# Trainium2 study: one branch removed between two layers, three adaLN blocks moved, one scatter replaced by one-hot products

## The chip, the cores and the metric

The kernel runs on one core of one Trainium2 chip. The metric is the device time of one execution in microseconds. The kernel before takes 1316.8 us (median of three runs, 1316.08 to 1317.06).

## What is computed

Two layers of a post-norm backbone over 256 context tokens and 256 latent tokens, width 1024. Each layer modulates its stream with adaLN vectors, projects it once to 4096 columns, feeds two head groups (a two-way gated linear recurrence, HGRN2, and a neighbourhood attention), projects back, normalises, and sends every token to 2 of 16 experts:

```python
def grouped_moe(h, w_router, b_router, w_gate_l, w_up_l, w_down_l):
    ...
    combine = jnp.sum(jax.nn.one_hot(e_idx, N_EXPERTS, dtype=f32) * gates[..., None], axis=1)
    out = jnp.zeros((n, shp[-1]), f32)
    for e in range(N_EXPERTS):
        hid = jax.nn.silu(t @ w_gate_l[e]) * (t @ w_up_l[e])
        out = out + combine[:, e:e + 1] * (hid @ w_down_l[e])
...
for l in range(DEPTH):
    mod_lat = (silu_c @ w_ada[l] + b_ada[l])[:, None, :]
    ...
    u_lat = (x_lat * (1.0 + sc1) + sh1) @ w_in[l]
    ...
    x_lat = layer_norm(ALPHA * x_lat + g1 * y_lat, ln1_g[l], ln1_b[l])
    f_lat = grouped_moe(x_lat * (1.0 + sc2) + sh2, ...)
    x_lat = layer_norm(ALPHA * x_lat + g2 * f_lat, ln2_g[l], ln2_b[l])
    ...
```

All data is float32. Layer 0 computes context and latent tokens (512), layer 1 the latent output alone (256).

## The kernel before

**A layer.** `run` calls `layer(l)` for l = 0 and 1. `layer` calls `front` (input projection, recurrence, attention, output projection), then `moe`, and for layer 0 `combine`, which gathers the experts' outputs, updates the stream `x`, normalises it, and writes layer 1's input (`xh`, `xl`). A list scheduler reorders the instructions of each engine; the source order and data dependences are what it starts from.

**The front.** The projection is cut into 16 chunks of 256 output columns. One chunk's weights are one load of 1 MB (`wload`, L199), issued on SP into a tile of the pool tag `w8`. That tag has three tiles (NWP = 3), handed out in turn. A loaded chunk is split in four pieces of 128x512 into a high part `wh` (ACT, L421) and a low part `wl` (L422, on POOL, or on DVE where the table SPL says V), and multiplied in three passes (xh·wh, xl·wh, xh·wl: L426, L427, L428, tiles `pscm` or `pstm`). A chunk has two units of 24 passes. Between the chunks stand pieces of the recurrence (`hgB` L727, `hgX` L744) and of the attention (`ats` L881, `atp` L901, `ato` L912).

**The adaLN blocks.** The adaLN vectors of both layers need 48 blocks of weights, 1 MB each. `fill(n)` computes the next n of them at a chosen chunk: eight calls on TensorE (L377, tile `psada`, 16 passes of 128x256 in the trace), a copy on ACT (L380), two small products (L384, `ptada`) and two small DVE instructions (L395, which write `ada`). In the front the blocks' weights go through the same three `w8` tiles. FILL0 and FILL1 are tables of n by chunk. Six blocks (NADA) of layer 1 that layer 0's front has left over are loaded at the end of layer 0's expert phase (L1486, tiles `wa`) and computed in one `fill(NADA, True)` behind the last expert.

**The experts.** Experts come in order 0 to 15. `gu(e, k0)` and `gu(e, k1)` are the two halves of gate and up (L1369, `pgA`), `htrans` transposes the hidden tile (L1394, `pth`), `down(e)` multiplies by the second matrix (L1406, `pdA`) and evicts the result to `y` (ACT L1419). POOL then scatters the rows of `y` to the DRAM buffer `yD` with an indirect DMA (L1433), two rows for each token. Weights stream in 1 MB loads through 16 slots (7 `we`, 3 `w8`, 6 `mw`).

**The layer's end.** If some expert has more tokens than its slots, a flag is read into a register and `If(fv)` (L1531) branches to `overflow`. The branch stands on every engine after each layer. Only then come `combine`'s loads of `yD` (L1555, eight of 512 KB on SP). For each of the eight y tiles `pair` weights one of a token's two rows on ACT (L1579) and adds the other on DVE (L1580). TensorE transposes the sums (L1568, `ptf`), DVE adds them to x (L1570), TensorE sums squares and means (L1052, `st`), POOL takes the power for the standard deviation (L1072), TensorE spreads it, and DVE normalises (L1086, L1087).

## Time and profile before

| what | value |
|---|---|
| median of the runs | 1316.8 us |
| profiled execution | 1317.83 us, of it the span 1316.1 us |
| TensorE busy in the span | 1199.3 us, 91% |
| VectorE, ScalarE, GpSimd busy | 45%, 31%, 25% |
| mean granted clock of TensorE | 0.958 |
| DMA | 339.32 MB, 258 GB/s over the span |

The profiled execution takes 1.73 us more than its span, which is what lies around the instructions that the profile shows, and 1.03 us more than the median of the runs. TensorE is busy for nine tenths of the time, so what matters are the places where it is not, and the stretches in which its work stands on the path to the end.

### The profile page before, as it was taken

The page shows a single profiled execution, that of the slowest core. Times are in us where ns is not written, and L with a number is a line of the kernel's source. Part 1 is how long each engine was busy: PE and PEld are TensorE (multiplying, and loading weights), DVE is VectorE, ACT ScalarE, POOL GpSimd, SP SyncE. Part 2 cuts the span into 40 slices and gives each one's busy share as a digit, 9 for nine tenths or more (in the row PEclk, how much of TensorE's full clock was granted, in tenths as well). Part 3 has the DMA queues.
Part 4 walks back from the last instruction along what each step waited for, and adds up shares of the span by engine and source line. Part 5 has one row for each costly group of instructions (what it writes and reads, how often), then busy time and mean ns, then how long its engine had stood idle before and what let it go on. Part 6 is the DMA issues. An engine that isn't in the chain of part 4 may idle for free. (4 is left out here: it accounts for less than half of the span.)

```text
span 1316.1 us, 22763 instructions
## 1 busy us (share of the span) xinstructions
PE 1199.3 (91%) x8919; PEld 747.6 (57%) x8919; DVE 590.2 (45%) x1397; ACT 413.8 (31%) x905; POOL 334.4 (25%) x349
## 2 busy tenths in 40 slices
PE   6989999988999799998997999998889899999984
PEld 4778767667788334333332688876667734333321
DVE  2466554786735414121111756364785524322214
ACT  2233254452544114111112653354345312001011
POOL 2233243323223101111000534353343311111001
PEclk9999999999999799999998999998999889999996
DMA  8794325313385799999998524354335799999993
GB/s 299 250 313 189 122 89 197 116 52 108 124 332 188 266 374 375 386 395 384 412 404 298 227 101 167 115 192 152 131 116 213 314 352 380 389 404 402 421 413 151
DMA packets 67684, 339.32 MB, mean 258 GB/s; under 512 B 10003, under 2 KB 17907, under 8 KB 31856
## 3 DMA queue, kind: packets, MB, share of 16 engines
q1 hardware_dynamic: 54016, 315.74, 62.1%
q0 software_dynamic: 5936, 12.58, 2.9%
q10 hardware_dynamic: 7616, 9.44, 2.2%
q8 instruction: 74, 1.21, 0.4%
q14 instruction: 42, 0.34, 0.1%
HBM read 322.80 MB, written 20.45 MB: 261 GB/s over the span
## 5 line engine op out<-in xcount | busy, mean ns | idle before, releaser
L422 POOL TENSOR_TENSOR wl<-w,wh 128x512 fp32r<-128x512 f32 x121 | 166.4, 1389 | 188.5 <-ACT wh L421 171.7
L1369 PE MATMUL pgA<-we,xgT 128*64 128x512 f32 x688 | 165.2, 613 | 2.7 <-DMA we<-in_wgu_dram 2.7
L426 PE MATMUL pscm<-xh,wh 128*128 128x512 f32 (+1 forms) x320 | 119.1, 376 | 3.3 <-ACT wh L421 2.3
L427 PE MATMUL pscm<-xl,wh 128*128 128x512 f32 (+1 forms) x320 | 120.7, 379 | 0.7 <-POOL xl L1603 0.5
L428 PE MATMUL pscm<-xh,wl 128*128 128x512 f32 (+1 forms) x320 | 118.6, 375 | 2.8 <-POOL wl L422 2.6
L421 ACT ACTIVATE wh<-w 128x512 fp32r<-128x512 f32 x160 | 96.5, 626 | 50.4 <-PE pscm L427 18.7
L1369 PEld LDWEIGHTS pgA<-we,xgT 128*64 128x64 f32 x688 | 48.1, 140 | 95.1 <-issue 84.9
L427 PE MATMUL pstm<-wl,xh 128*128 128x256 f32 x320 | 92.6, 290 | 3.4 <-DVE wl L422 1.8
L428 PE MATMUL pstm<-wh,xl 128*128 128x256 f32 x320 | 91.9, 287 | 0.0
L426 PE MATMUL pstm<-wh,xh 128*128 128x256 f32 x320 | 91.6, 287 | 0.0
L1433 POOL DMA_INDIRECT yD<-y,ss x25 | 23.0, 921 | 244.6 <-DVE y L1421 79.9
L1406 PE MATMUL pdA<-we,hdT 128*64 128x512 f32 x320 | 77.6, 619 | 3.3 <-DMA we<-in_wd_dram 3.2
L1369 PE MATMUL pgA<-mw,xgT 128*64 128x512 f32 x336 | 77.5, 598 | 0.0
L1360 DVE COPY xgT<-ptx 128x256 f32<-128x256 f32 (+1 forms) x32 | 15.4, 482 | 134.2 <-PE ptx L1354 91.1
L426 PEld LDWEIGHTS pscm<-xh,wh 128*128 128x128 f32 x320 | 61.3, 193 | 13.8 <-ACT wh L421 2.4
L428 PEld LDWEIGHTS pscm<-xh,wl 128*128 128x128 f32 x320 | 61.5, 193 | 12.5 <-POOL wl L422 3.4
L427 PEld LDWEIGHTS pscm<-xl,wh 128*128 128x128 f32 x320 | 61.9, 194 | 11.2 <-POOL xl L1603 1.6
L1387 DVE SCALAR_TENSOR_TENSOR hid<-hid,pgA 128x256 f32<-128x256 f32 x32 | 13.5, 421 | 115.2 <-ACT hid L1386 115.1
L427 PEld LDWEIGHTS pstm<-wl,xh 128*128 128x128 f32 x320 | 61.4, 192 | 5.4 <-POOL wl L422 2.2
L1386 ACT ACTIVATE hid<-pgA 128x256 f32<-128x256 f32 x32 | 12.3, 383 | 159.5 <-PE pgA L1369 159.5
L428 PEld LDWEIGHTS pstm<-wh,xl 128*128 128x128 f32 x320 | 61.5, 192 | 1.1 <-issue 0.8
L426 PEld LDWEIGHTS pstm<-wh,xh 128*128 128x128 f32 x320 | 61.4, 192 | 0.5
(394 smaller groups left out, 2358.9 us busy)
## 6 DMA issues: line engine op xcount, KB each, us to landing
we<-in_wgu_dram SPq DMA_DIRECT2D x86, 1024.0 KB
mw<-in_wgu_dram SPq DMA_DIRECT2D x42, 1024.0 KB
w<-in_wada_dram SPq DMA_DIRECT2D x41, 1024.0 KB
we<-in_wd_dram SPq DMA_DIRECT2D x40, 1024.0 KB
w<-in_win_dram SPq DMA_DIRECT2D x29, 1024.0 KB
mw<-in_wd_dram SPq DMA_DIRECT2D x24, 1024.0 KB
w<-in_wout_dram SPq DMA_DIRECT2D x11, 1024.0 KB
wa<-in_wada_dram SPq DMA_DIRECT2D x6, 1024.0 KB
```

Source lines behind the costliest of these rows:

```text
L421: self.nc.scalar.activation(hi, src, AF.Copy)
L422: leng.tensor_tensor(lo, src, hi.bitcast(F32), op=ALU.subtract)
L426: mm(out, lh, rh, start=first, stop=False, **k)
L427: mm(out, lh, rl, start=False, stop=False, **k)
L428: mm(out, ll, rh, start=False, stop=last, **k)
L1360: V.tensor_copy(t[:, 0:4, :c], src)
L1369: mm(pA[64 * j:64 * j + 64, :], xgT[e][:, k, 0:64], wk[:, 512 * j:512 * j + 512], start=(k == 0), stop=(k == KT - 1), skip_group_check=Tru ...
L1386: S.activation(h, ps[:, :n], AF.Tanh, scale=0.5)
L1387: V.scalar_tensor_tensor(h, h, 1.0, ps[:, :n], op0=ALU.add, op1=ALU.mult)
L1406: mm(dA[64 * j:64 * j + 64, :], hdT[e][:, kb, 0:64], wk[:, 512 * j:512 * j + 512], start=(kb == 0), stop=(kb == 3), skip_group_check=True, ...
L1433: G.indirect_dma_start(out=self.yD[l][:], out_offset=bass.IndirectOffsetOnAxis(ap=idx, axis=0), in_=y[:c], in_offset=None, bounds_check=2 ...
```

## The change

The change has five parts.

1. `layer(0)` no longer reads its flag or branches. The flag is kept in `over`, merged with layer 1's, and one `If` at the end of the program reruns both layers on the slow path (not taken with these inputs).
2. FILL0 rises from 2 to 3 at chunks 8, 11 and 13, and behind layer 0's experts NAFTER = 3 blocks are computed where NADA = 6 were. The three weights tiles there are now `we` tiles.
3. `early` now holds for layer 0 too: expert 14's second matrix is loaded before the second half of expert 15's first, and `down(14)` stands ahead of `gu(15, k1)`.
4. Expert 15's 64 rows of layer 0 aren't scattered. They are weighted by their gate on ACT and DVE (`yh`, `yl`, L1430 and L1431 of the changed kernel), and `pair` adds them through 16 products of 128x512 with a one-hot matrix `place` (`pz`, L1636). `last_slots` builds `place` while expert 13 is computed. The addition in `pair` becomes: DVE L1638 (eight, one operand from PSUM), DVE L1643 (six), ACT L1640 (two) and POOL L1641 (two).
5. `pairs_load`, the eight loads of `yD`, is issued ahead of `down(15)`; it depends on the scatters of experts 0 to 14 alone. `pair(1, 1)` stands ahead of `end(0)`.

```diff
+NAFTER = 3
-FILL0 = (0, 0, 0, 2, 2, 2, 2, 0, 2, 0, 2, 2, 0, 2, 0, 2)
+FILL0 = (0, 0, 0, 2, 2, 2, 2, 0, 3, 0, 2, 3, 0, 3, 0, 2)
...
+        with tc.If(self.fv):
+            self.slow = True
+            self.x = [self.xtile(h) for h in range(2)]
+            for l in range(2):
+                self.l = l
+                self.layer(l)
...
+            if l == 0 and e == NE - 1:
+
+                yh, yl = self.yparts = [self.rt([P, 512], "hr", 4, F32R) for _ in range(2)]
+                S.activation(yh[:], dA[:], AF.Copy, scale=self.slots[:, 0:1])
+                V.scalar_tensor_tensor(yl[:], dA[:], self.slots[:, 0:1], yh[:].bitcast(F32), op0=ALU.mult, op1=ALU.subtract)
+                return
...
-            early = l == 1 and e == NE - 2
+            early = e == NE - 2
...
-                for i in range(NADA):
-                    if i < NWP:
-                        w = self.wp.tile([P, 2048], F32, tag="w8", name="wa")[:]
-                    else:
-                        w = ep.tile([P, 2, 1024], F32, tag="mw", bufs=NMW, name="wa").rearrange("p a b -> p (a b)")
-                    nc.sync.dma_start(w, self.A["wada"][self.todo[i][:2]])
-                    self.todo[i] = self.todo[i][:2] + (w,)
+                for i in range(NAFTER) if self.todo else ():
+                    t = self.todo[i][:2]
+                    w = self.wep.tile([P, 2, 1024], F32, tag="we", bufs=NWE, name="wa").rearrange("p a b -> p (a b)")
+                    nc.sync.dma_start(w, self.A["wada"][t])
+                    self.todo[i] = t + (w,)
+                self.pairs_load()
...
-            self.fill(NADA, True)
+            self.fill(NAFTER, True)
         else:
             self.finish()
-        with self.tc.If(fv):
-            self.overflow(l)
...
+    def last_slots(self, r):
...
+        for i, x in enumerate((R["oh1"], R["oh2"], R["q1"])):
+            V.tensor_tensor(w, x[:, :T, NSTAT:], mine, op=ALU.mult)
+            V.tensor_reduce(g[:, i], w, axis=AX.X, op=ALU.add)
...
+        for n in range(T):
+            oh = rt([P, 256], "rs", 2)[:, :P].rearrange("p (j s) -> p j s", j=2)
+            V.tensor_scalar(oh, self.iota16[:, :64].unsqueeze(1).to_broadcast([P, 2, 64]), g[:, 2, n:n + 1], None, op0=ALU.is_equal)
+            nc.tensor.matmul(ps[:, 0:2], oh.rearrange("p j s -> p (j s)"), gv[:, n], start=(n == 0), stop=(n == T - 1))
...
+        rows = rt([P, 512], "hr", 4)
+        nc.sync.dma_start(rows[:], self.A["const"][:, _C["rowtok"][0]:])
+        self.place = rt([P, 512], "hr", 4, F32R)
+        V.tensor_scalar(self.place[:], rows[:], self.slots[:, 1:2], None, op0=ALU.is_equal)
...
         def pair(h, cc):
             y = ys[2 * h + cc]
+            js = slice(64 * cc, 64 * cc + 64)
             for i in range(2):
-                g = self.R["gt"][:, :, 2 * h + i]
-                S.activation(y[:, i, 0], y[:, i, 0], AF.Copy, scale=g[:, 0:1])
-                V.scalar_tensor_tensor(y[:, i, 0], y[:, i, 1], g[:, 1:2], y[:, i, 0], op0=ALU.mult, op1=ALU.add)
+                n = 2 * h + i
+                ps = self.bank(2 * cc + i if h == 0 else 6 + i, "pz")
+                for k, part in enumerate(self.yparts):
+                    mm(ps[:], self.place[js, 128 * n:128 * n + 128], part[js, :], start=(k == 0), stop=(k == 1), tile_position=(64 * cc, 0))
+                g = self.R["gt"][:, :, n]
+                V.scalar_tensor_tensor(y[:, i, 0], y[:, i, 0], g[:, 0:1], ps[:], op0=ALU.mult, op1=ALU.add)
+                if (h, i) == (1, 1):
+                    S.activation(y[:, i, 1], y[:, i, 1], AF.Copy, scale=g[:, 1:2])
+                    G.tensor_tensor(y[:, i, 0], y[:, i, 0], y[:, i, 1], op=ALU.add)
+                else:
+                    V.scalar_tensor_tensor(y[:, i, 0], y[:, i, 1], g[:, 1:2], y[:, i, 0], op0=ALU.mult, op1=ALU.add)
```

**Order, place 1: SP's loads around chunk 8.** A name's first number counts the `w8` tiles in turn; tile n shares its memory with tile n + 3. Before, chunk 8's two blocks are 22 and 23, and chunk 9's weights are 24:

```order
L199 DMA w8_22_1814<-in_wada_dram 128x2048
L199 DMA w8_23_1824<-in_wada_dram 128x2048
L199 DMA w8_24_1841<-in_win_dram 128x2048
L199 DMA w8_25_1947<-in_win_dram 128x2048
L199 DMA w8_26_2021<-in_wada_dram 128x2048
```

In the changed kernel:

```order
L200 DMA w8_22_1815<-in_wada_dram 128x2048
L200 DMA w8_23_1825<-in_wada_dram 128x2048
L200 DMA w8_24_1835<-in_wada_dram 128x2048
L200 DMA w8_25_1852<-in_win_dram 128x2048
L200 DMA w8_26_1958<-in_win_dram 128x2048
```

Chunk 9's weights have moved from place 24 to place 25, which shares its memory with block 22.

**Order, place 2: TensorE from chunk 8 to chunk 9.** In the changed kernel, with tile numbers as above (tile 1854 and its neighbours are pieces of chunk 9's weights):

```order
L387 MATMUL psada<-w_22_1815,scw 32x256
L924 MATMUL ato<-pT,bv_604 64x256 x7
L387 MATMUL psada<-w_22_1815,scw 32x256 x7
L387 MATMUL psada<-w_23_1825,scw 32x256 x8
L387 MATMUL psada<-w_24_1835,scw 32x256 x8
L394 MATMUL ptada<-ct,adasb 128x4 x2
L436 MATMUL pscm<-xh_0_119,wh_1854 128x512
```

Before, the same place reads as follows:

```order
L377 MATMUL psada<-w_22_1814,scw 32x256
L912 MATMUL ato<-pT,bv_603 64x256 x7
L377 MATMUL psada<-w_22_1814,scw 32x256 x7
L377 MATMUL psada<-w_23_1824,scw 32x256 x8
L384 MATMUL ptada<-ct,adasb 128x4 x2
L426 MATMUL pscm<-xh_0_118,wh_1843 128x512
```

One block has been added; nothing else has moved between the blocks and chunk 9's first pass.

**Order, place 3: TensorE and VectorE at the end of layer 0.** Before, on TensorE, from the middle of `down(14)` to the branch:

```order
L1394 MATMUL pth<-ct,hid_6441 128x128 x2
L1406 MATMUL pdA<-mw,hdT_6431 64x512 x4
L1406 MATMUL pdA<-mw,hdT_6468 64x512 x8
L377 MATMUL psada<-wa,scw 32x256 x24
L1525 TENSOR_LOAD flag_4734
L1531 COMPARE_AND_BRANCH
```

In the changed kernel, from the first half of `gu(15)` to the first transposes of the combination:

```order
L1381 MATMUL pgA<-we,xgT_6355 64x512 x8
L1418 MATMUL pdA<-mw,hdT_6488 64x512 x8
L1381 MATMUL pgA<-mw,xgT_6355 64x512 x8
L1406 MATMUL pth<-ct,hid_6514 128x128 x2
L1418 MATMUL pdA<-mw,hdT_6521 64x512 x8
L1636 MATMUL pz<-hr_6555,hr_6451 128x512 x3
L387 MATMUL psada<-wa,scw 32x256 x8
L1636 MATMUL pz<-hr_6556,hr_6451 128x512 x2
```

After seven more rows of `pz` (12 of the 16 in all), the last 16 calls of `psada` and `ptada`, the transposes `ptf` follow. The load of the flag and the branch are gone, and `pth` of expert 15 now has no other product behind it before `down(15)`.

On VectorE of the changed kernel, from the remainder `yl` on:

```order
L1431 SCALAR_TENSOR_TENSOR hr_6556<-pdA,slots_6446,hr_6555 128x512
L1638 SCALAR_TENSOR_TENSOR y<-y,gt_3579,pz 128x512
L405 SCALAR_TENSOR_TENSOR ada_77<-ptada,bada 128x6 x2
L1643 SCALAR_TENSOR_TENSOR y<-y,gt_3579 128x512
L1638 SCALAR_TENSOR_TENSOR y<-y,gt_3579,pz 128x512
L1643 SCALAR_TENSOR_TENSOR y<-y,gt_3579 128x512
L1638 SCALAR_TENSOR_TENSOR y<-y,gt_3579,pz 128x512
L1624 SCALAR_TENSOR_TENSOR x_78<-ptf,ada_76,x_78 128x256
```

The adaLN instruction L405 stands between the first y tile's two additions, so the first `ptf` comes behind `ptada`.

## Rows read from the trace of the kernel before

**Rows 1.** Windows: stretch, its length, busy us (x count) by engine, clock, DMA share, GB/s.

```profile
0.00:330.00 330.00, 299.52 (x2377) 231.41 (x2378) 192.50 (x398) 125.99 (x264) 103.39 (x104) 0.98 0.49 174
456.00:692.00 236.00, 230.48 (x1715) 87.00 (x1711) 49.91 (x114) 45.91 (x106) 25.28 (x27) 0.99 1.00 390
1056.00:1290.00 234.00, 223.06 (x1426) 82.95 (x1428) 59.95 (x129) 27.03 (x70) 27.17 (x29) 0.98 1.00 395
```

**Rows 2.** Timeline of PE, chunk 8 to chunk 9: start us, us, what.

```profile
189.59 0.62 PE L377 MATMUL psada<-w,scw 128*32 128x256 f32 x2
...
192.01 1.93 PE L377 MATMUL psada<-w,scw 128*32 128x256 f32 x30
...
194.34 0.48 PE L426 MATMUL pscm<-xh,wh 128*128 128x512 f32 x1
...
199.90 0.39 PE L426 MATMUL pscm<-xh,wh 128*128 128x512 f32 x1
```

**Rows 3.** Timeline of SP's DMA queue, then of ACT, 165 to 218 us.

```profile
170.76 22.26 SPq L199 DMA_DIRECT2D w<-in_win_dram  x2
...
208.60 0.33 SPq L199 DMA_DIRECT2D w<-in_win_dram  x1
...
214.36 1.68 ACT L421 ACTIVATE wh<-w 128x512 fp32r<-128x512 f32 x3 [2.19 <-DMA w<-in_win_dram]
```

**Rows 4.** Groups by line, 185 to 216 us: busy us, mean ns, idle before.

```profile
L422 POOL TENSOR_TENSOR wl<-w,wh 128x512 fp32r<-128x512 f32 x7 | 9.1, 1308 | 10.9 <-PE pscm L428 5.8 <-ACT wh L421 5.1
```

**Rows 5.** Timeline of PE, the blocks at chunks 11 and 13.

```profile
241.49 1.92 PE L377 MATMUL psada<-w,scw 128*32 128x256 f32 x28
...
245.17 0.50 PE L426 MATMUL pscm<-xh,wh 128*128 128x512 f32 x1
...
296.24 1.50 PE L377 MATMUL psada<-w,scw 128*32 128x256 f32 x22
...
299.49 0.38 PE L426 MATMUL pstm<-wh,xh 128*128 128x256 f32 x1
```

**Rows 6.** Timeline of PE, end of layer 0.

```profile
689.74 3.60 PE L1369 MATMUL pgA<-mw,xgT 128*64 128x512 f32 x16
...
695.00 0.44 PE L1394 MATMUL pth<-ct,hid 128*128 128x128 f32 x2
...
698.64 3.65 PE L1406 MATMUL pdA<-mw,hdT 128*64 128x512 f32 x16 [1.34 <-ACT y L1419]
702.23 2.80 PE L377 MATMUL psada<-wa,scw 128*32 128x256 f32 x48
709.26 5.49 PE L377 MATMUL psada<-wa,scw 128*32 128x256 f32 x48 [4.24 <-PEq L1531]
...
719.18 2.32 PE L1568 MATMUL ptf<-ct,y 128*128 128x128 f32 x8 [3.29 <-DVE y L1580]
```

**Rows 7.** Timelines of POOL, SP's queue and DVE, end of layer 0.

```profile
698.87 0.90 POOL L1433 DMA_INDIRECT yD<-y,ss  x1 [9.07 <-ACT y L1419]
705.48 0.90 POOL L1433 DMA_INDIRECT yD<-y,ss  x1 [5.72 <-ACTq L1531]
...
712.60 5.16 SPq L1555 DMA_DIRECT2D y<-yD  x8
...
715.92 0.25 DVE L395 SCALAR_TENSOR_TENSOR ada<-ptada,bada 128x12 f32<-128x12 f32 x2 [21.23 <-PE ptada L384]
718.33 0.75 DVE L1580 SCALAR_TENSOR_TENSOR y<-y,gt 128x512 f32<-128x512 f32 x1 [2.16 <-ACT y L1579]
...
738.23 0.69 DVE L1086 TENSOR_TENSOR x<-x,prn 128x512 f32<-128x512 f32 x1 [1.13 <-PE prn L1080]
```

**Rows 8.** Windows: the later half of layer 0's combination.

```profile
726.00:734.00 8.00, 7.59 (x51) 3.63 (x49) 6.29 (x16) 5.77 (x14) 0.00 (x0) 1.00 0.96 395
```

**Rows 9.** Groups by line and form, DVE, 170 to 330 us.

```profile
L837 DVE TENSOR_TENSOR rot<-rot,rots 128x256 f32<-128x256 f32 x6 | 2.5, 421 | 5.3 <-POOL rots L835 5.3
L836 DVE TENSOR_TENSOR rot<-pscm,ct 128x256 f32<-128x256 f32 x6 | 2.5, 413 | 0.0
```

**Rows 10.** Windows: a gap in layer 0's expert phase and the stretch behind it.

```profile
613.00:619.00 6.00, 1.01 (x8) 0.34 (x5) 1.26 (x3) 0.66 (x2) 0.06 (x1) 0.99 1.02 322
619.00:622.00 3.00, 3.00 (x13) 1.47 (x13) 0.00 (x0) 0.00 (x0) 0.93 (x1) 0.50 1.02 365
```

More of the change, by code (lines that the diff above doesn't have):

```diff
@@ L311, in run @@
         self.late = self.open_step = None
+        self.over = c([P, 1], "over")
+        self.slow = False
         for l in range(2):
@@ L452, in layer @@
         self.moe(l)
+        if self.slow:
+            self.overflow(l)
         self.close(moe)
@@ L487, in blocks @@
             def blocks(p):
-                for b in (2 * p, 2 * p + 1):
+                for b in (2 * p, 2 * p + 1) if self.todo else ():
                     self.todo[b - self.todo[0][1]] = (l, b, self.wload(A["wada"][l, b])[:])
@@ new lines, in pairs_load @@
+    def pairs_load(self):
+        nc, NTL, yD = self.nc, self.T * P, self.yD[0]
+        ys = []
+        for h in range(self.T // 2):
+            for cc in range(2):
+                y = self.wep.tile([P, 2, 1024], F32, tag="we", bufs=NWE, name="y").rearrange("p n (j c) -> p n j c", j=2)
+                src = yD[0:2 * NTL, :].rearrange("(j n p) c -> n p j c", j=2, p=P)
+                for i in range(2):
+                    nc.sync.dma_start(y[:, i], src[2 * h + i][:, :, 512 * cc:512 * cc + 512])
+                ys.append(y)
+        self.ys = ys
@@ L1538, in combine @@
         NTL = self.T * P
-        a, yD = self.ada[l], self.yD[l]
+        a = self.ada[l]
         self.lazy = []
```

50 lines of the change are left out of this document (31 added, 19 removed).

## The prediction, made before the changed kernel was run

> **What bounds the kernel now.** I read the windows first. In layer 0's front TensorE is busy 299.5 of 330 us, in layer 0's experts 230.5 of 236, in layer 1's experts 223 of 234 with the DMA engines busy throughout [rows 1]. So a microsecond added to or taken from TensorE's path in the front or between the layers reaches the end nearly whole: no later stretch has slack to take it up. The change touches two such places, and I read each in the timeline.
>
> The first is chunk 8 of layer 0's front. There TensorE goes without a gap from the two adaLN blocks (189.59 and 192.01 us) into chunk 9's first pass at 194.34, and to that chunk's second unit at 199.90 [rows 2]. Chunk 9's weights were issued at 170.76, 23 us ahead of use, and the load after it only at about 193 (the row's two loads span 22.26 us), just when chunk 8's blocks let go of their `w8` tiles [rows 2, 3].
>
> The second is the end of layer 0. TensorE stops at 705.03 (702.23 + 2.80), waits 4.24 us at the branch, does the other 48 passes of adaLN in 5.49 us where the same number took 2.80 before the gap, and waits 3.29 us again for the first y [rows 6]. The y loads are late because expert 15's scatter itself waits for the branch: it is issued at 705.48, and SP issues the loads at 712.60, 7.1 us later, when it has landed. The first addition comes 5.7 us after that, at 718.33, the first normalisation at 738.23 [rows 7].
>
> **The change, part by part.**
>
> *Moving three blocks.* 48 passes of 2.80 us are three blocks [rows 6], 0.93 us each. Three more in the front cost 2.8 us of TensorE.
>
> *The wait at chunk 9.* In the order, chunk 9's weights now share memory with the first of chunk 8's three blocks, so their load can't be issued until that block has been multiplied. Its 16 passes are the two at 189.59 and 14 of the 30 at 192.01; 14/30 of 1.93 us is 0.90, so it is done at 192.9 [rows 2]. From issue to the first split a lone load took 5.8 us (208.60 to 214.36) [rows 3]; its 1.05 MB alone would take 2.7 us at the 390 GB/s of the expert phase [rows 1]. Those are the ends; I take 5.2, near the row that is a whole load. The first `wh` piece takes 0.56 (1.68 for three) [rows 3]: the first pass is at 192.9 + 5.2 + 0.56 = 198.7, where TensorE would be free at 194.34 + 0.93 = 195.3. The idle time is 3.4 us. Then the unit goes at the pace of POOL, which needs 1.31 us for a `wl` piece [rows 4], against 5.56 us for 24 passes in four pieces [rows 2]: four pieces from 198.7 end at 203.9, and two passes more make 204.4. Against 199.90 that is +4.5 with the block in it; the ends are +2.0 and +5.1.
>
> *Chunks 11 and 13.* The same tile sharing holds for the weights of chunks 12 and 14. At chunk 11 the first block is done at about 242.3 (12 of the 28 passes from 241.49), the weights can be used at 242.3 + 5.8 = 248.1, and TensorE, with the block, is free at 245.17 + 0.93 = 246.1 [rows 5]. The scheduler has moved one `hgX` and some `ats` ahead, work that is merely brought forward; I give it 1 us. So +0.9 for the block and +1.0 of idle time. At chunk 13 the first block ends at about 296.7 (6 of 22 passes from 296.24), the weights can be used at 302.5, TensorE is free at 299.49 + 0.93 + 1 = 301.4 [rows 5]: +0.9 and +1.1, of which the recurrence's own waits there may hide half. I take +1.9 and +1.5 (0.9 each at least, 2.5 at most). A group at chunk 10 now splits in two for another +0.2.
>
> The front's sum is 4.5 + 1.9 + 1.5 + 0.2 = **+8.1**. Of waits so placed some part vanishes in later waits of the recurrence; I take +7.5, with +4.0 (2.0, twice 0.9, 0.2) and +10.3 (5.1, twice 2.5, 0.2) as ends.
>
> *The end of layer 0.* TensorE's work on experts 14 and 15 is unchanged up to `down(15)`, but `down(14)` no longer covers expert 15's hidden tile. That chain took from 693.34 (689.74 + 3.60) to the end of `pth` at 695.44, and its eviction follows [rows 6]: about 2.6 us, so `down(15)` starts near 699.6 instead of 698.64 and ends at 703.3. One block (0.9), twelve `pz` (0.23 a pass of 128x512 from 5.56/24: 2.8 us) and two blocks (1.9) lead to 709.0. From the last `psada` to DVE's `ada` took 1.2 us (714.75 to 715.92) [rows 6, 7]: `ada` is at 710.2, one more addition of 0.75 follows [rows 7], and the first `ptf` stands at 711.2. The y loads must not be later than that: expert 14's scatter, issued at 698.87 before, now comes earlier, since `down(14)` ends some 3.9 us sooner; I take 697, landing 7.1 us later at 704.1, the first y at 709.8 (712.60 to 718.33 was 5.7) [rows 7]. So `ada` and y are ready together, and **the first ptf moves from 719.18 to about 711.3, a lead of 7.9**.
>
> *What the lead is worth at the norm.* Between first `ptf` and first norm lie 19.05 us now [rows 6, 7]. DVE gets eight L1638 and six L1643 where it had eight L1580 at 0.75 (0.70 from start to start): six more, +4.2 us. ACT and POOL lose or gain work that nobody waits for, unless POOL's power comes behind three `wl` splits (3.9 us [rows 4]), as its order has it. TensorE has four more `pz` there (0.9). If the gaps of DVE and TensorE hid all of this 5.1, the lead would stay 7.9; if none, it is 2.8, and with the splits as well it turns into a loss of 1.1. Late in the combination DVE has 1.7 us of 8 free, TensorE 0.4 [rows 8]; so less than half can hide. I take 3.2 as paid: **-4.7**, ends +1.1 and -7.9.
>
> Here a rule of the Trainium skill can be held against a row. DVE took 413 ns for an addition with one operand in PSUM and 421 ns for one with both in SBUF, same shape [rows 9]: no difference, so I price L1638 like L1580. The Trainium skill, page "Perfetto Trace Analysis", section "Optimizing Scalar/DVE Operations", gives DVE an overhead of about 60 ns on SBUF and 125 ns on PSUM; by it eight L1638 would cost another 0.5 us (an estimate from that page), and the net would be 0.5 higher. The rows don't show it.
>
> *Nothing else on the path.* Building `place` is small DVE work in the expert phase, where DVE is busy 50 of 236 us [rows 1]; if its cover failed, it would delay a hidden tile by under 1 us. The 256 KB of constants and the three megabytes moved off the end are not what TensorE waits for at the layer's end [rows 6]. The branch at the end stays.
>
> **Sum.** +7.5 - 4.7 = **+2.8 us**. The profiled execution would go from 1317.83 to 1320.6; the median of the runs, 1.0 lower, from 1316.8 to **1319.6**.
>
> **The rivals.**
>
> *A, faster: the lead reaches the norm.* If TensorE and y arrival, not DVE, pace the combination, the six added instructions fall into DVE's waits, and 7.9 us arrive whole. For it: DVE waits for ACT, `ptf` or a DMA several times between 718 and 738. Against it: DVE has to finish all eight pairs before the sums close. It decides once over two thirds of the added 5.1 us is hidden and the front's loads take the shorter time: 4.0 - 7.9 = -3.9, **1312.9**.
>
> *B, no change: chunk 9's tile is not the one that is held.* If the three-tile rotation frees a tile earlier than the order's names say, the front costs only its blocks, 2.8 + 0.2 = 3.0, and 3.0 - 4.7 = -1.7, **1315.1**. For it: nothing in the trace shows the new rotation. Against: SP's load near 193 already follows the blocks in just this way [rows 3].
>
> *C, slower still: the clock falls in the new gaps.* Behind a gap in the experts TensorE's clock was 0.50 for 3 us, that is 1.2 instead of 2.4 GHz [rows 10]; such a stretch loses 1.5 us. After the gaps at chunks 9 and 14 it could do so twice: 2.8 + 3 = +5.8, **1322.6**. Against: those gaps are 3.4 us and less, that one about 5.
>
> **How the numbers follow.** About 0.2%, 2.6 us, is what a measurement can tell from no change. The forecast with its spread has 0.48: its upper three fifths count as slower (0.30), the rest as the same (0.18). A has 0.30 (faster), B 0.07 (same), C 0.15 (slower). So faster 0.30, same 0.25, slower 0.45. The extremes are 4.0 - 7.9 = -3.9 and 10.3 + 1.1 = +11.4; holding eight in ten, I cut the upper one, where both bad ends must meet, at +7.7, and let the lower reach 1.4 past A, for loads that come still sooner: **1311.5 to 1324.5**. The forecast's own range is 1317 to 1323.
>
> **What would show it.** Right: chunk 9's weights issued on SP near 193 instead of 171, TensorE idle 2 to 4 us ahead of chunk 9's first `pscm` and 1 us ahead of chunks 12 and 14, the recurrence's end and the expert phase some 7 us later; at the layer's end no wait at a branch, y loads some 8 us earlier against `down(15)`, and DVE nearly gapless from the first addition to the power. Wrong: no gap at chunk 9 (B), or DVE still waiting for `ptf` or y while the norm leads by 7 us or more (A), or a clock of 0.5 after 198 us (C).

## The result, and the profile after

The changed kernel takes **1338.4 us** (median of four runs, 1335.45 to 1339.78), the kernel before 1316.9 in the same runs: a ratio of **1.0156**, 95% interval [1.0133, 1.0179]. It is slower by some 21 us where the prediction said +2.8, and its range ended at 1324.5. The sign was right, the size wrong by a factor of more than seven.

| | before | after |
|---|---|---|
| profiled execution, its span | 1317.83, 1316.1 us | 1338.85, 1336.7 us |
| first psada of chunk 8 | 189.59 | 185.19 |
| first psada of chunk 11 | 239.07 | 243.00 |
| first psada of chunk 13 | 293.39 | 301.50 |
| first psada of chunk 15 | 352.42 | 365.51 |
| first `pth` of expert 0 (experts begin) | 466.27 | 484.89 |
| `pth` of expert 14 (last part still alike) | 683.02 | 701.70 |
| first `ptf` | 719.18 | 733.05 |
| first `prn` (the norm) | 735.09 | 753.48 |
| start of the last `pfin` group | 1298.26 | 1313.44 |
| VectorE's last instruction ends | 1311.04 | 1326.22 |

All times are starts in the profiled executions, read off TensorE's timeline; the last line is off VectorE's. Subtracting neighbours splits the 20.6 us of the span into four: the front **+18.6** (466.27 to 484.89), the way from expert 14 to the norm **-0.3** (52.07 to 51.78), layer 1 **-3.2** (563.17 to 559.96, norm to last `pfin`), and the time behind VectorE's last instruction **+5.4** (5.06 to 10.48). The experts themselves are unchanged, as their windows show, the answer to [rows 1] moved by 18 and 16 us (the last window is 2 us longer than there):

```profile
0.00:330.00 330.00, 293.66 (x2341) 223.99 (x2342) 182.67 (x394) 123.02 (x259) 93.06 (x96) 0.97 0.51 182
474.00:710.00 236.00, 231.56 (x1720) 88.16 (x1721) 51.38 (x120) 46.52 (x107) 25.65 (x27) 0.99 1.00 390
1072.00:1308.00 236.00, 224.46 (x1423) 82.68 (x1425) 58.69 (x122) 26.72 (x69) 26.27 (x28) 0.98 0.99 392
```

In the front's 330 us TensorE is busy 5.9 us less (293.66 against 299.52) although three blocks were added to them, and gets less far: the gaps are new.

**The front.** Timeline of TensorE in the changed kernel from chunk 8 to 9, the answer to [rows 2]; in brackets stands the idle time ahead of an instruction and what ended it:

```profile
185.19 0.62 PE L387 MATMUL psada<-w,scw 128*32 128x256 f32 x2
187.61 2.79 PE L387 MATMUL psada<-w,scw 128*32 128x256 f32 x46
...
194.23 0.80 PE L436 MATMUL pscm<-xh,wh 128*128 128x512 f32 x1 [3.29 <-ACT wh L431]
...
196.19 0.63 PE L436 MATMUL pscm<-xh,wh 128*128 128x512 f32 x1
...
201.01 0.40 PE L436 MATMUL pscm<-xh,wh 128*128 128x512 f32 x1
```

The gap is there and has the size foreseen (3.29 us; 3.4 was predicted). What follows it was not in the sum: the passes take 0.63 us instead of 0.39 until about 200.6. The windows of the same stretch say why, in the column behind POOL's, the granted clock:

```profile
190.00:195.00 5.00, 1.71 (x12) 1.02 (x6) 0.93 (x3) 2.56 (x6) 0.74 (x1) 0.88 0.91 378
195.00:200.00 5.00, 4.86 (x12) 3.47 (x11) 0.00 (x0) 0.74 (x2) 4.24 (x4) 0.50 0.56 234
```

A clock of 0.50 is 1.2 GHz. The 12 passes in these 5 us would have been 21 or 22 at full clock (0.23 us from start to start in [rows 2]), and some 6.4 us at half clock lose about 3.

The cause of the gap is in the timelines of SP's queue and of ACT [rows 3]: chunk 9's weights, issued at 170.76 before, now go out only when the first block is done.

```profile
168.32 0.33 SPq L200 DMA_DIRECT2D w<-in_wada_dram  x1
188.72 1.19 SPq L200 DMA_DIRECT2D w<-in_win_dram  x2
...
193.55 2.19 ACT L431 ACTIVATE wh<-w 128x512 fp32r<-128x512 f32 x4 [2.06 <-DMA w<-in_win_dram]
```

At chunks 11 and 13 the same happens. The wait shows ahead of the `ats` passes that the scheduler had moved in front of the next chunk [rows 5]:

```profile
245.42 2.78 PE L387 MATMUL psada<-w,scw 128*32 128x256 f32 x44
...
253.19 0.36 PE L892 MATMUL ats<-ks,qs 128*128 128x256 f32 x1 [2.73 <-DMA ks<-ks]
...
303.92 2.79 PE L387 MATMUL psada<-w,scw 128*32 128x256 f32 x46
...
312.74 0.36 PE L892 MATMUL ats<-ks,qs 128*128 128x256 f32 x1 [3.77 <-ACT wh L431]
```

**Between the layers.** Timelines of TensorE, ACT, POOL and SP's queue in the changed kernel, the answer to [rows 6, 7]:

```profile
711.86 3.60 PE L1381 MATMUL pgA<-mw,xgT 128*64 128x512 f32 x16
718.93 0.41 PE L1406 MATMUL pth<-ct,hid 128*128 128x128 f32 x2 [3.47 <-DVE hid L1400]
719.81 5.16 PE L1418 MATMUL pdA<-mw,hdT 128*64 128x512 f32 x16 [0.47 <-ACT hdT L1408]
...
733.05 0.44 PE L1622 MATMUL ptf<-ct,y 128*128 128x128 f32 x1 [0.99 <-DVE y L1643]
...
753.48 0.71 PE L1092 MATMUL prn<-ct,lnst 128*128 128x128 f32 x4 [0.53 <-POOL lnst L1084]
...
716.27 1.20 ACT L1438 ACTIVATE y<-pdA 64x512 f32<-64x512 f32 x2 [10.96 <-DMA yD<-y,ss]
717.49 0.39 ACT L1398 ACTIVATE hid<-pgA 128x256 f32<-128x256 f32 x1
...
707.56 0.92 POOL L1451 DMA_INDIRECT yD<-y,ss  x1 [12.90 <-DVE y L1444]
717.74 0.90 POOL L1451 DMA_INDIRECT yD<-y,ss  x1 [9.26 <-ACT y L1438]
...
722.09 4.92 SPq L1591 DMA_DIRECT2D y<-yD  x8
```

No engine waits at a branch any more. But ACT, which empties `down(14)` into a y tile, waits for an earlier scatter to have read that tile (its idle time of 10.96 us is ended by `yD<-y,ss`; some 4 of it lie behind the end of `down(14)` at 712.02), and behind that instruction in ACT's queue stands expert 15's hidden tile. So TensorE waits 3.47 us, and `down(15)` then runs at half clock, 5.16 us for 16 passes against 3.65 [rows 6].

**The end.** All entries on the line of the rerun's branch; the numbers behind the colon are the shortest, median and longest duration in ns, the last two the first and last start:

```profile
L321 SPq EVENT_SEMAPHORE  x9: 17/17/17, 1329.5 to 1331.9; - x9
L321 POOLq EVENT_SEMAPHORE  x5: 17/42/43, 1326.7 to 1327.0; - x5
L321 PEldq COMPARE_BRANCH  x1: 3421/3421/3421, 1314.0 to 1314.0; - x1
L321 PEldq EVENT_SEMAPHORE  x1: 51/51/51, 1319.0 to 1319.0; - x1
L321 ACTq COMPARE_BRANCH  x1: 54/54/54, 1321.7 to 1321.7; - x1
L321 POOLq COMPARE_BRANCH  x1: 58/58/58, 1324.0 to 1324.0; - x1
L321 ACTq EVENT_SEMAPHORE  x1: 17/17/17, 1324.5 to 1324.5; - x1
L321 DVEq COMPARE_BRANCH  x1: 72/72/72, 1325.4 to 1325.4; - x1
L321 SPq COMPARE_BRANCH  x1: 53/53/53, 1326.6 to 1326.6; - x1
L321 DVEq EVENT_SEMAPHORE  x1: 21/21/21, 1328.8 to 1328.8; - x1
L321 POOLq INC_SWDGE_SEM  x1: 1424/1424/1424, 1329.3 to 1329.3; - x1
```

The comparison itself takes 0.05 to 0.07 us on ACT, POOL, DVE and SP. With these inputs every engine then jumps over the branch's body. The next instruction comes 2.8 us later on ACT (1321.7 to 1324.5) and 3.4 on DVE (1325.4 to 1328.8); part of that is the engine's own last work, and behind the end of that work it is 2.1 us on ACT, 1.9 on POOL and 2.6 on DVE. In the kernel before the two flags' branches look like this:

```profile
L1531 DVEq COMPARE_BRANCH  x2: 56/64/72, 694.9 to 1310.0; - x2
L1531 DVEq EVENT_SEMAPHORE  x2: 21/21/21, 695.1 to 1311.1; - x2
L1531 PEldq COMPARE_BRANCH  x2: 3797/4365/4933, 704.2 to 1298.7; - x2
L1531 PEldq EVENT_SEMAPHORE  x2: 51/51/51, 709.2 to 1303.8; - x2
```

There DVE goes on 1.1 us later at the program's end (1310.0 to 1311.1), under 0.1 us behind its last work, and 0.2 us later between the layers. On TensorE's queue (PEldq) the next entry comes 5.0 or 5.1 us after the branch at all three places (704.2 to 709.2, 1298.7 to 1303.8, 1314.0 to 1319.0). The code jumped over is now a whole second pass over both layers. The program ends with a closing instruction of POOL that takes 5.1 to 5.2 us in both kernels: before, it starts 0.1 us behind POOL's last work (1309.7), in the changed kernel 6.0 us behind it (1330.8). The jump is 1.9 us of that; the rest lies up to the end of the semaphore entry of 1.42 us at 1329.3, which stands on the branch's line.

### The profile page after: what moved, and what is told of

The parts are those of the page before. It is cut to its first block, busy times and chain, and to the rows that moved or that the text cites. A ratio compares the mean times of both kernels' runs of the same rounds, so it can differ in the third digit from the quotient of the medians.

```text
span 1336.7 us, 22819 instructions
## 1 busy us (share of the span) xinstructions
PE 1209.4 (90%) x8946; PEld 754.9 (56%) x8946; DVE 594.8 (44%) x1423; ACT 411.0 (31%) x899; POOL 335.3 (25%) x350
## 5 line engine op out<-in xcount | busy, mean ns | idle before, releaser
L1381 PEld LDWEIGHTS pgA<-we,xgT 128*64 128x64 f32 x688 | 48.3, 140 | 96.2 <-issue 86.0
L438 PEld LDWEIGHTS pscm<-xh,wl 128*128 128x128 f32 x320 | 61.8, 194 | 10.8 <-POOL wl L432 1.5
```

What stands on the lines that cost most here:

```text
L438: mm(out, ll, rh, start=False, stop=last, **k)
L1381: mm(pA[64 * j:64 * j + 64, :], xgT[e][:, k, 0:64], wk[:, 512 * j:512 * j + 512], start=(k == 0), stop=(k == KT - 1), skip_group_check=Tru ...
```

## The experiments

Ratios are to the kernel before, run on the same chip in turn, with 95% intervals. "Front" is the first `pth` of expert 0 against 466.27, "stretch" the time from expert 14's `pth` to the first `prn` (52.07 before, 51.78 after), both from one profiled execution each. One execution's front is not sharp: in nine kernels below, of either design, with the three blocks at chunks 7, 9 and 12 it comes out between +1.8 and +10.8. The way from the first `psada` of chunk 8 to that of chunk 15 repeats better: 162.8 us before and with the blocks undone, 178.6 to 180.3 in five kernels with third blocks at chunks 8, 11 and 13, and 163.2 to 167.6 in the nine.

### Which part costs: the blocks undone, the blocks alone

In the changed kernel, three blocks back behind layer 0:

```diff
-NAFTER = 3
+NAFTER = 6
...
-FILL0 = (0, 0, 0, 2, 2, 2, 2, 0, 3, 0, 2, 3, 0, 3, 0, 2)
+FILL0 = (0, 0, 0, 2, 2, 2, 2, 0, 2, 0, 2, 2, 0, 2, 0, 2)
...
```

> The changed kernel with the three adaLN blocks moved back (FILL0 as before, six blocks behind layer 0's experts). Theory: the late weight loads at chunks 9, 12 and 14 cost some 15 to 18 us of the changed kernel's 21, so without them layer 0's expert phase begins where it did before (first pth of expert 0 near 466 us) and the time is 1321 to 1324 us; what is left over 1317 is the longer tail behind the last store (5.4 us in the trace of the changed kernel) less a small gain between the layers. Rival: the front is slower because of the changed program as such (new order, longer code), not because of the blocks; then the time stays at 1333 to 1338 us.

Measured: **1.0031** [1.0004, 1.0058]; front +1.3, stretch 54.1.

In the kernel before, the blocks moved and nothing else (FILL0 of the changed kernel, NAFTER = 3 in place of NADA):

> The kernel before with nothing changed but the three blocks moved (FILL0 new, three blocks behind the experts). Theory: late weights, idle TensorE and the half clock behind it cost 15 to 18 us in the front, three blocks fewer at the half clock between the layers give back 2.7: 1329 to 1333 us, with chunk 9's weights issued about 20 us later than before. Rival (the blocks cost only their own TensorE time, 2.8 us, and the rest of the front's loss came from other parts): 1316 to 1319 us.

Measured: **1.0102** [1.0069, 1.0135]; front +19.5, stretch 47.0. What follows: the front's loss comes with the block positions alone, and undoing them takes back four fifths of the change's loss (1.0156 to 1.0031). The same three blocks shorten the stretch by 5.1 us in the old design, where the prediction had counted TensorE's passes alone; in the changed kernel they are worth 2.3 (54.1 against 51.8).

### The branch at the end

In the changed kernel, without it; the rerun for more than the expected number of tokens is left out here, and in two later kernels:

```diff
-        with tc.If(self.fv):
-            self.slow = True
-            self.x = [self.xtile(h) for h in range(2)]
-            for l in range(2):
-                self.l = l
-                self.layer(l)
```

> The changed kernel without the branch at the program's end; it leaves out the rerun that the branch guards, which these inputs don't take. Theory: the jump over the rerun's code costs the tail 5.4 us more than the jump over the overflow code did, so the time falls by at least 5.4 us, to 1333 or less; if the short jump before had a cost of its own at the end too, to 1329. The time from the last DVE instruction to the span's end falls from 10.5 us to 5 or less. Rival: the long tail is the end of the program as such (POOL's drain of 5.1 us stands there in both), then the time stays within 1.5 us of 1338.

Measured: **1.0119** [1.0066, 1.0172], 4.9 us less than with it by the ratios (0.0037). The interval is wide, so the place decides: from VectorE's last instruction to the end of the span it is 4.5 us (1319.06 to 1323.6), with the rerun 10.5. In the later pair it is 8.7 and 4.5. Over all kernels here it is 8.3 to 10.8 with the rerun (eight kernels), 4.7 to 5.1 with the old branch (six) and 4.5 to 4.6 with none (three).

### Where the blocks stand

In the changed kernel, the third blocks at chunks 7, 9 and 12, where none stood:

```diff
-FILL0 = (0, 0, 0, 2, 2, 2, 2, 0, 3, 0, 2, 3, 0, 3, 0, 2)
+FILL0 = (0, 0, 0, 2, 2, 2, 2, 1, 2, 1, 2, 2, 1, 2, 0, 2)
```

> The changed kernel with the same three blocks, but one each at chunks 7, 9 and 12, where none stood, instead of a third at 8, 11 and 13. No chunk's weights then share a tile with a block of the chunk just ahead that is multiplied only at its end. Theory (tile turn): the gaps ahead of chunks 9, 12 and 14 vanish, the front costs only the blocks' 2.8 us, and the time is 1321 to 1326 us. Rival (three more blocks in the front cost this much wherever they stand, through DMA or the scheduler's order): 1333 to 1338 us.

Measured: **1.0057** [1.0025, 1.0089]; front +2.7, stretch 49.3. Its windows across chunk 9's start:

```profile
190.00:195.00 5.00, 5.00 (x47) 3.66 (x40) 3.22 (x7) 2.86 (x5) 0.00 (x0) 1.00 0.93 306
195.00:201.00 6.00, 6.00 (x29) 4.95 (x28) 2.58 (x7) 1.98 (x4) 0.74 (x1) 1.00 0.65 269
```

TensorE is busy throughout and the clock stays at 1.00: with the same three blocks in the same front, neither gap nor half clock here. From chunk 8 to chunk 15 it takes 163.4 us against 180.3. So most of the cost is not the blocks' work, but which weights' tile they hold.

The same positions in the kernel before:

> The kernel before, branch and scatter as they were, with three blocks moved from the layer's end into the front, one each at chunks 7, 9 and 12. Theory: the front costs 2.8 us more (the blocks alone), the layer's end gains 5 (three blocks fewer behind the branch at the half clock; the run with only the blocks moved showed the stretch from expert 14's pth to the first prn fall from 52.1 to 47.0): 2 us faster than before, ratio 0.997 to 0.9995. Rival (the end waits for y in any case, what the blocks free is lost in that wait): 1 to 3 us slower, ratio 1.001 to 1.002.

Measured: **0.9998** [0.9979, 1.0017]; front +7.1, stretch 47.0. The stretch is as the theory has it; the front lost more in this execution than the blocks' 2.8, and the ratio lies between theory and rival. And one site by itself, a third block at chunk 8 alone in the kernel before (NAFTER = 5):

> The kernel before with one block moved, the third at chunk 8 (FILL0 3 at chunk 8 alone, five blocks behind the experts). It shows one of the three places by itself. Theory (late weights, then the half clock): TensorE idles 3.3 us ahead of chunk 9's first pass and the passes of that chunk run at the half clock behind it, so the way from chunk 8's first psada to chunk 10's takes 34 us instead of 26.7; the layer's end gains 1.7 (a third of the 5.1 that three blocks gave): 4 to 6 us slower than before, ratio 1.003 to 1.005. Rival (only all three together do harm, by the recurrence's order further down): ratio 0.999 to 1.001.

Measured: 1.0016 [0.9998, 1.0034], less than the 1.003 to 1.005 expected; front +6.5, stretch 50.0. TensorE's timeline has the gap of the changed kernel again:

```profile
195.60 0.80 PE L427 MATMUL pscm<-xh,wh 128*128 128x512 f32 x1 [3.30 <-ACT wh L422]
```

From the first psada of chunk 8 to that of chunk 11 it takes 57.5 us, against 49.5 before and 57.8 in the changed kernel (185.19 to 243.00): one site costs 8 us up to there, of which 3.4 are back by chunk 15. Here the windows from 245 to 260 and 305 to 322 have the full clock; in the changed kernel the latter shows 0.80.

### The stretch between the layers

`early` for layer 1 only, in the changed kernel:

```diff
-            early = e == NE - 2
+            early = l == 1 and e == NE - 2
```

> The changed kernel, but layer 0 again computes expert 15's second half of gate and up ahead of expert 14's down product (early for layer 1 alone). In the changed kernel's trace ACT's eviction of expert 14's y waited 11 us for the landing of scatter 13 (one y tile), and expert 15's hidden tile stood behind it in ACT's queue: TensorE idled 3.5 us and ran down(15) at the half clock. Theory (y tile): with the old order the hidden tile comes first and its chain is covered by down(14), the gap ahead of down(15) falls from 4 us to about 1.3 and the stretch from expert 14's pth to the first prn, 51.8 us in the changed kernel, becomes 48 to 50: 1334 to 1337 us. Rival (the gap is the hidden tile's own chain, and the y loads, which then wait for a later scatter 14, take back what is won): 51 to 53 us, 1338 or more.

Measured: 1.0123 [1.0092, 1.0154]; stretch 48.2, 3.6 shorter than with it. Expert 14's y in a tile of its own, with `early` on (in this kernel expert 15 has no y tile):

```diff
-            y = et([P, D], "y")
+            if l == 0 and e >= NE - 2:
+                y = ep.tile([P, 2, 1024], F32, tag="mw", bufs=NMW, name="y")[:, 0]
+            else:
+                y = et([P, D], "y")
```

> The changed kernel, with the y of layer 0's expert 14 in a tile of its own (a weights tile that is free by then), so that its eviction doesn't wait for scatter 13. Theory (y tile): ACT evicts y of expert 14 some 4 us sooner, expert 15's hidden tile comes 2 us sooner, TensorE's gap ahead of down(15) shrinks to about 2.5 us, the y loads are issued 3 to 4 us sooner against down(15), and the stretch from expert 14's pth to the first prn falls from 51.8 to 48 to 50 us: 1334 to 1336 us. Rival: the combination is paced by DVE's 14 additions alone, then the first ptf comes sooner and the first prn does not (51 to 52 us).

Measured: 1.0098 [1.0065, 1.0131]; stretch 48.5, 3.3 shorter. Timelines of TensorE and ACT there:

```profile
716.12 0.41 PE L1406 MATMUL pth<-ct,hid 128*128 128x128 f32 x2 [1.48 <-DVE hid L1400]
717.01 3.65 PE L1418 MATMUL pdA<-mw,hdT 128*64 128x512 f32 x16 [0.47 <-ACT hdT L1408]
...
714.68 0.38 ACT L1398 ACTIVATE hid<-pgA 128x256 f32<-128x256 f32 x1 [2.19 <-PE pgA L1381]
```

The wait ahead of `pth` falls from 3.47 to 1.48 and `down(15)` is back at 3.65: 2.0 and 1.5 us, together the 3.3 within 0.2. Both edits take the same thing away, one by not moving `down(14)` ahead, one by giving it a free tile; the order itself, then, is worth nothing once its tile is free. How much the tile costs depends on the clock: in the kernel with the blocks spread and nothing else changed the wait ahead of `pth` is 2.48 us, `down(15)` takes 3.65, the stretch is 49.3, and the free tile gains only 1.1 there (48.3, below).

The free tile in the kernel before, with the spread blocks:

> As the kernel before with the blocks spread to chunks 7, 9 and 12, and besides layer 0's last two y tiles in tiles of their own. Before, ACT's eviction of expert 15's y waited 5.4 us for scatter 13's landing, and scatter, landing and y loads hang behind it. Theory: the scatter of expert 15 is issued 1.5 to 2.5 us sooner and the first ptf with it, so another 1.5 to 2.5 us: ratio 0.995 to 0.998. Rival: the scatter waits for the branch on ACT and POOL anyway (705.48 before), no change against the spread blocks alone.

Measured: 1.0024 [1.0005, 1.0042], stretch 51.8 against 47.0 without it. Here SP's queue has a load of layer 1's weights at 715.06 ahead of the y loads at 715.51, and the first `ptf` waits 8.38 us for y: the edit changed the order of the loads too, so this run, which missed theory and rival, says nothing on the tile.

Both cures in the changed kernel, then without the branch as well:

> The changed kernel with the blocks at chunks 7, 9 and 12 and expert 14's y in a tile of its own, the two changes that helped it alone (1.0156 to 1.0057 and to 1.0098). If they add up: 1.0156 - 0.0099 - 0.0058 = 0.9999, no slower than before. Rival: both act on the same wait, then 1.004 to 1.006.

> As the run with the blocks spread and the second y tile, and without the branch and the rerun at the end (left out: the slow path, which these inputs don't take). If the three costs add up, 1.0156 - 0.0099 - 0.0058 - 0.0037 = 0.9962: what the changed kernel's idea would be worth if its rerun cost nothing. Rival (the jump was hidden behind what these two changes moved): 0.9999 as with the branch.

Measured: **1.0021** [1.0000, 1.0042], stretch 48.3; without branch **0.9980** [0.9959, 1.0000], stretch 48.3. The two cures take back 0.0135 of 0.0156, and the branch 0.0041 (5.4 us) more. No kernel run here that computes everything is faster than the one before by more than its interval; the nearest is the one before with the spread blocks, at 0.9998. The levels of the two came out some 0.002 above what was expected of them.

### Are the megabytes at the layer's end on the path?

In the kernel before with the spread blocks, three loads of adaLN weights put back, into tiles that nothing reads; no arithmetic is added (the diff is against that kernel):

```diff
-                for i in range(NAFTER):
+                for i in range(NADA):
...
-                    nc.sync.dma_start(w, self.A["wada"][self.todo[i][:2]])
+                    nc.sync.dma_start(w, self.A["wada"][self.todo[min(i, NAFTER - 1)][:2]])
...
```

> The kernel before with the blocks spread to chunks 7, 9 and 12 (ratio 0.9998), but with six loads of adaLN weights behind the experts as before, of which three feed nothing. It separates the two things that moving blocks took off the layer's end: 48 passes of TensorE and 3 MB of DMA. Theory (DMA): scatter 15 took 3.6 us to land with three loads and 7.1 with six, y waits for it, so with the dead loads it takes 6 to 7 us again, and the stretch from expert 14's pth to the first prn goes from 47.0 back to 50 to 52 us: ratio 1.002 to 1.004. Rival (TensorE): the stretch stays at 47 to 48 us, ratio 0.9998.

Measured: 1.0027 [1.0006, 1.0047], against 0.9998; stretch **52.9** against 47.0. POOL's last scatter and SP's y loads, first without the three loads, then with:

```profile
710.85 0.90 POOL L1434 DMA_INDIRECT yD<-y,ss  x1 [4.10 <-ACTq L1532]
...
714.48 6.16 SPq L1556 DMA_DIRECT2D y<-yD  x8
```

```profile
709.71 0.90 POOL L1434 DMA_INDIRECT yD<-y,ss  x1 [5.75 <-ACTq L1533]
...
717.19 4.71 SPq L1557 DMA_DIRECT2D y<-yD  x8
```

From the scatter to the loads that wait for its landing it takes 3.6 us without and 7.5 with them; the kernel before had 7.1 [rows 7]. So the scatter's few rows land 3.9 us later with 3 MB more ahead of them. The scatter itself is issued later too, 22.5 us behind expert 14's `pth` and not 20.8: ACT, which empties expert 15's product, waits 5.46 us there for an earlier scatter's landing. Together this is the stretch's gain of 5 us, with no pass of TensorE added.

### Are the added additions what the combination waits for?

From first `ptf` to first `prn` it takes 15.9 us before and 20.4 in the changed kernel and in the one with both cures. To take VectorE's six additions away, expert 15's product was put by TensorE straight into the PSUM tiles of the transposes (this and the next kernel change expert 15's part of the output):

```diff
...
+                for m, part in enumerate(self.yparts):
+                    mm(pt[:, 0:256], part[js, cs], self.place[js, 256 * hf:256 * hf + 256], start=False, stop=(m == 1),
+                       skip_group_check=True, tile_position=(64 * (k // 4), 0))
...
```

> Edit: the run with the third blocks spread over chunks 7, 9 and 12 and expert 14's y in a tile of its own, and now expert 15's one-hot product goes straight into the PSUM tiles of the transposes (TensorE accumulates it there), so that VectorE has its 8 additions of before and ScalarE its 8 scalings, and none of the six added additions. Theory (the 4.5 us that the way from the first ptf to the first prn gained, 15.9 to 20.4 us, are those six additions): the way falls to 16 to 17 us, the stretch from expert 14's pth to the first prn from 48.3 to 44 to 46 us, and the ratio from 1.0021 to 0.9985 to 1.0000. Rival (something else holds the way, the loads of layer 1's weights that the end waits for or TensorE's half clock): the way stays at 19 to 21 us, or it falls and the stretch stays at 48 us all the same, and the ratio is 1.0010 to 1.0040.

> Edit: as the run before it, without the branch at the end and the rerun behind it (the path for more than the expected number of tokens is left out). The branch was worth 4.9 and 5.4 us in two pairs of runs. Theory: the ratio lies 0.0035 to 0.0045 under that of the run before it, at 0.9945 to 0.9965, and the time from VectorE's last instruction to the span's end is 5 to 6 us and not 10 to 11. Rival (the two gains do not add, since with the boundary shorter the end waits for a transfer): the difference is under 0.002.

Measured: 1.0196 [1.0168, 1.0224], without branch 1.0121 [1.0096, 1.0146]. The first run's theories both missed. The way grew to 36.9 us (717.55 to 754.42). The 32 passes of 64x256 take 0.58 us each, by the trace's entries for their line, and the window of the stretch has TensorE busy and the clock down:

```profile
717.00:757.00 40.00, 38.77 (x121) 17.39 (x122) 12.85 (x29) 13.10 (x27) 4.25 (x4) 0.51 0.36 141
```

TensorE stays at half clock for 40 us. The two kernels' distance, 0.0075 (0.0035 to 0.0045 was expected), is uncertain by 0.004; behind VectorE's last instruction they take 8.3 and 4.6 us. The edit made another engine the bound, so it cannot speak for the additions. The next one takes them away and adds nothing, with the products still computed; POOL's two additions go too, and expert 15's part is missing from the output:

```diff
-                V.scalar_tensor_tensor(y[:, i, 0], y[:, i, 0], g[:, 0:1], ps[:], op0=ALU.mult, op1=ALU.add)
...
+                S.activation(y[:, i, 0], y[:, i, 0], AF.Copy, scale=g[:, 0:1])
+                V.scalar_tensor_tensor(y[:, i, 0], y[:, i, 1], g[:, 1:2], y[:, i, 0], op0=ALU.mult, op1=ALU.add)
```

> Edit: the run with the blocks spread and expert 14's y in a tile of its own (ratio 1.0021, stretch 48.3 us, first ptf to first prn 20.4 us), with TensorE's one-hot products of expert 15 kept and their addition into y left out: VectorE has its 8 additions of before and ScalarE its 8 scalings. Expert 15's part is missing from the output. Theory (the 4.5 us that this way gained are VectorE's six added additions): it falls to 16 to 17 us, the stretch to 44 to 45.5 us, and the ratio to 0.9985 to 1.0000. Rival (it is TensorE's clock in the gap, or the transfers that layer 1's start waits for): the way stays at 19 us or more, or what it loses comes back as a longer wait ahead of the first ptf, the stretch stays at 47.5 us or more, and the ratio at 1.0010 to 1.0035.

Measured: the way **15.8** us (720.87 to 736.68), the stretch **44.8** (691.91 to 736.68). Windows of the way, with the additions and without:

```profile
721.00:742.00 21.00, 18.81 (x94) 7.80 (x94) 17.33 (x33) 9.39 (x22) 8.00 (x9) 0.84 0.65 259
```

```profile
721.00:737.00 16.00, 15.24 (x87) 7.22 (x87) 11.64 (x27) 10.33 (x23) 2.40 (x4) 0.89 0.77 307
```

VectorE (the third busy number) has 5.7 us less to do, and the way is 4.6 shorter. Of the ways measured with the additions in place, 20.4 to 21.1 us, none comes near. The theory holds in the stretch. The time does not show it: **1.0016** [0.9991, 1.0040], against 1.0021. Layer 1, from the norm to its first expert's `pth`, takes 340.2 us here and 335.3 with the additions (736.68 to 1076.89, 742.13 to 1077.38), and one place of it is seen: 195 us behind the norm a window of 15 us has a clock of 0.77 here and 1.00 there. This way takes 333 to 343 us in the kernels of this document, and 338.7 in the one with both cures and no branch, whose code up to there is the same as with it; so the 4.9 us can be a difference between two executions. Why the clock fell in one and not in the other was not tried.

## Why the prediction was wrong

**The front, +7.5 predicted, +18.6 measured: the step that failed most.** The mechanism was right in each part that the prediction could name: the loads issued when the first block is done, a gap of 3.3 us, sites at chunks 9, 12 and 14. Three sizes were off. From chunk 8 to chunk 15 the way grew by 17.5 us where the sum had 8.1.

- Chunk 9 was given +4.5; from chunk 8 to chunk 10 the changed kernel loses 7.6 (189.59 to 216.31 became 185.19 to 219.50). The first pass came 4.3 us later relative to the blocks (9.04 against 4.75), just as worked out (3.4 idle and 0.93 for the block). The other 3.3 is, but for some 0.3, the half clock, which the prediction held as rival C and priced at 1.5 us a gap, from a stretch of 3 us in [rows 10]; here it lasted twice as long.
- Chunks 11 and 13 were given 1.9 and 1.5; the ways from chunk 11 to 13 and 13 to 15 grew by 4.2 and 5.0. The block's 0.93 was right; the idle time was 2.73 and 3.77 us where the sum had 1.0 and 1.1. The term that was too small is the weights' arrival: from issue to the first split the loads took 6.1 and 6.5 us (246.52 to 252.62, 305.04 to 311.51) and not 5.8, and the 0.56 of that split, which chunk 9's sum has, was left out here. The `ats` brought forward wait as well, but end their wait (253.19, 312.74) about when the first piece is there (253.2, 312.1), so they add 0.7 at most. Behind chunk 13's gap the clock fell too (0.76 from 308 to 318).
- The prediction took 0.6 off, for waits that would swallow the loss; none is seen up to chunk 15. From chunk 10 to 11 it is another 0.7, and from chunk 15 to the experts another 5.5 us went (365.51 to 484.89 against 352.42 to 466.27). With 7.6, 4.2 and 5.0 that makes 23.0, and chunk 8 was reached 4.4 us earlier in this execution: +18.6. The 5.5 is not shown to be the delay's: from chunk 15 to the experts all sixteen other kernels take 117.4 to 119.8 us, the one with the blocks undone 117.4, and the one execution of the kernel before stands alone with 113.85. Measured against the blocks undone, 2.0 of it are left.

Rival C thus named the clock, which was missing from the sum, with +5.8 in all; it had 0.15. Rival B (tile not held) is out: the gap was there. Rival A (faster) needed the lead of 7.9 us to reach the norm, where 0.3 arrived.

**"The branch at the end stays": +5.4 unforeseen.** The instruction stays, the code behind it does not: the kernel before jumps over layer 1's overflow path, the changed one over a rerun of both layers, and behind its last work ACT goes on 2.1 us later, POOL 1.9 and DVE 2.6, where it took under 0.1 each. On POOL the branch's semaphore entries follow, so its closing instruction starts 6.0 us behind its last work and not 0.1. Three pairs of runs, with and without branch, give 4.9, 5.4 and 9.9 us, each uncertain by 4 to 8; the traces' 3 to 6 us at the program's end (8.3 to 10.8 with the rerun against 4.7 to 5.1) are the better measure. This was shown by leaving branch and rerun out together; neither the length of the code nor the semaphore entries were varied by themselves. The Trainium skill, page "Runtime: NRT & Kernel Launch", section "Instruction fetch mechanics", says that a taken branch whose target isn't in the two pages of instructions that are held has to fetch the target's page before it goes on. The trace agrees in sign: ACT, POOL and DVE pause by the 1.9 to 2.6 us above. The page gives no time for it.

**The boundary, -4.7 predicted, -0.3 measured.** Its parts are -5.1, +3.3, +4.5 and, as what remains, -3.0.

- Three blocks fewer: -5.1 (52.07 to 46.98), where the prediction had counted TensorE's 2.8 us of passes and declared the three megabytes "not what TensorE waits for". The dead loads show that they were: TensorE waits for y, y for a scatter, and the scatter lands later with the megabytes ahead of it. The 5.1 is the old design's; in the changed kernel the same blocks are worth 2.3 (54.1 against 51.8), so these parts do not simply add.
- The y tile: +3.3 (1.1 where the clock holds), missed. The order shows `down(14)` ahead of `gu(15, k1)` on TensorE, and the prediction followed TensorE alone. ACT's queue has y ahead of the hidden tile, and y's tile was still being read by a scatter.
- The additions: 3.2 was taken as paid of 5.1; the way grew by 4.5, and the run without the additions gives back 4.6. VectorE's queue hides next to nothing there. POOL's three splits, which the prediction feared ahead of the power, cost next to nothing: they end at 752.61, and the power's last input on VectorE at 752.62.
- What remains, 3.0, is argued to be what the change does remove, the branch's wait and the last scatter; it was not measured by itself, and with 2.3 for the blocks it would be 5.8. The lead of the first `ptf` was 4.8 and not 7.9 (719.18 + 18.68 - 733.05, where 18.68 is by how much expert 14's `pth` is later); the y tile's 3.3 are the rest.

Gain and price of the new addition nearly cancel: with the same three blocks the old design needs 47.0 us here, the new one 48.3 once y has its free tile. That DVE's price per addition was right shows in the rows: L1638, with an operand in PSUM, takes 0.75 us, and L1643 without one 0.74 (DVE's timeline of the changed kernel). The Trainium skill, page "Perfetto Trace Analysis", section "Optimizing Scalar/DVE Operations", gives VectorE a longer overhead on PSUM than on SBUF; these rows don't show it either.

**Layer 1, 0 predicted, -3.2 measured.** The loss was expected to reach the end whole. From the norm to the last `pfin` it takes 554 to 563 us in these runs, and the kernel before stands at the upper end, so the -3.2 lies within what single executions differ by. What sets this was not settled.

## What to carry to other kernels

Before filling a place with one more piece of work, see whose tile it takes: work that fits in TensorE's time can still hold back the load of the next weights, and the gap costs its length and, as behind chunk 9, a stretch at half clock after it. When the order of one engine is changed, read the queues of the engines that serve it for the same place; the wait that appears is often in one of these. And a branch whose body is not run still has a price beyond its comparison: behind its last work VectorE went on within 0.1 us at the old closing branch and after 2.6 us at the one over the rerun, POOL got semaphore entries to pass, and the program's end came 3 to 6 us later. Which of these comes from the length of the body was not shown.

## What the runs showed that was not expected

- After a gap of 3.29 us TensorE worked at 1.2 GHz for some 6.4 us. In the combination of the run with the products in the transposes it was busy 38.8 of 40 us and the granted clock was 0.51 throughout; 128-row passes and transposes alternate there with 64-row passes in short groups. Why the clock didn't rise was not tried.
- A scatter's time to landing was 3.6 us, or 7.5 with 3 MB more of plain loads issued ahead of it, and this held up the end of a layer.
- Moving the same three blocks to neighbouring chunks takes the ratio from 1.0156 to 1.0057.
